# State-space core of a four-layer trunk: output products in 32-column pieces, a new order of products, scans and copies, and two steps of a table computation moved up in the gating layer

## The chip, the cores and the metric

The kernel runs on one core of one Trainium2 chip. The time is that of one execution on the device, in microseconds (us); lower is better. Kernels are compared by the median of several runs on the same chip.

The core's engines work side by side, each on its own queue of instructions in program order: TensorE (PE in the profile, its weight loads PEld), VectorE (DVE), ScalarE (ACT), GpSimd (POOL), and SyncE (SP), which here only issues transfers. An instruction that waits holds up everything behind it on its engine.

## What is computed

The reference is a trunk of four residual layers on 256 tokens of 1024 features in float32. Layer i has a token mixer (attention, spatial gating, state space, attention again) and then a gated MLP with a short convolution. Cut to the two mixers that the change touches:

```python
def chunked_spatial_gating(xn, w_in, v_norm_g, w_s, b_s, w_o):
    u, v = jnp.split(jax.nn.gelu(xn @ w_in), 2, axis=-1)
    v = rmsnorm(v, v_norm_g)              # 128-token chunks, 8 groups
    sv = jnp.einsum('gts,bcsgd->bctgd', jnp.tril(w_s), v) + b_s
    return (u * sv) @ w_o

def s5_layer(xn, w_in, lam_re, lam_im, log_dt, b_re, b_im, c_re, c_im, d_skip, w_glu):
    u = xn @ w_in                         # 64 groups of 16 features, 64 complex states each
    a = exp(dt * (lam_re + 1j * lam_im))  # and bbar from a, lam and b
    x[t] = a * x[t-1] + bbar @ u[t]       # over 256 tokens, by an associative scan
    y = real(c @ x[t]) + d_skip * u[t]
    a, g = jnp.split(gelu(y) @ w_glu, 2, axis=-1)
    return a * sigmoid(g)
```

## The kernel before

Every large product is made of three products of rounded operands (high by high, high by low, low by high): lines 126 to 128 where the weights are loaded into the array and tokens stream, lines 134 to 136 the other way about. A weight chunk of 1 MB comes from memory by an SP transfer (L42) into one of three `raw` buffers; ACT rounds it to the high part (L73, two halves) and DVE subtracts to get the low part (L74, two halves). `prep_to(n)` emits these for all chunks up to n, and `take()` hands out the next chunk. A raw buffer goes to a later chunk once both halves of L74 have read it; the transfer of a chunk is emitted up to two chunks ahead of the one that is being rounded. Chunks marked "tab" are tables of the state-space layer that the kernel has computed itself and stored in memory; they are only transferred (L56).

**The spatial gating layer** (`GMLP`). `body` masks a weight on POOL (L694), makes the last products of v, calls `vnorm` for two halves of the tokens (each has one POOL instruction, L165, for the reciprocal root), and then alternates products (`u`, `sv`, `down`) with `step()`. `step()` rounds weights and takes two steps of a generator, `self.bg`. In this layer that generator is `S5.powers`: powers of the complex decay by repeated squaring, all of it on POOL (L906 to L933), six steps and a closing one. Its scratch tile `powt` lies in the buffer tagged "gb", and that buffer is next given to the norm weights of the following layer (`load_g`, L141). The norm of a layer (`norm`) adds the residual (L192), squares (L153), takes the root on POOL (L165) and scales by these weights (L157); its result is transposed on PE (L181).

**The state-space layer** (`S5`). The 64 groups are 32 pairs. The recurrence is cut into pieces of 4 tokens and 64 chunks. `U` holds the inputs by pair with the 4 tokens side by side (L1240 and L1242 copy it out of the accumulators, 16 copies for each half of the pairs). For four blocks i of eight pairs: `gmm(i)` makes the chunk inputs (L1157), `scan(i)` multiplies by a table of powers, runs two DVE scans (L1175), and multiplies back (L1167 to L1187, some on POOL) to the states x. `kmm(n)` and `kevac(n)` make the short kernel `kk` inside a piece for one half of the pairs (L1196, L1202, and 16 ACT copies at L1206). `ymm(i)` adds three groups of eight products (L1217): `kk` by `U`, and the real and the imaginary states by a table `PP`. Then 16 ACT instructions apply gelu and put the four tokens of a piece into their places (L1224), one copies the high part (L1227), and DVE makes the low part (L1228). `glu(i)` multiplies block i by gate weights into four accumulators; after the fourth, `gate(b)` on ACT and DVE (L1283 to L1285) makes the first half of the output, and four more `glu` make the second.

The tables lie, in the order of their transfers, as bb, p0, gt0, p1, gt1 (`sources`, L752). `gmm` reads gt0 or gt1, `kmm` reads bb and p0 or p1, `ymm` reads p0 or p1. At L1131 `load_t` brings the tables of powers for scans 1 to 3 into the buffers that held the normed input. `mg` (L1107), read by the scans, holds one of the three raw buffers until scan 3 has read it.

The order written out before is: kmm(0); copies of U, the first half on ACT and the second on DVE; gmm(0); scan(0); kevac(0); gmm(1); kmm(1); then for i = 1, 2, 3: scan(i), (kevac(1) after the first), ymm(i-1), gmm(i+1). Gate chunk 0 is rounded ahead of scan(3) (L1250). glu(0), ymm(3), glu(1), glu(2), glu(3) follow, with further chunks rounded by `step()` between them.

Of the kernel before, what the change touches and what calls it, by code (L numbers as in the profile page):

```python
# [8 lines left out]
F32 = mybir.dt.float32  # L9
F32R = mybir.dt.float32r  # L10
BF16 = mybir.dt.bfloat16
AF = mybir.ActivationFunctionType
# [3 lines left out]
D = 1024  # L16
# [600 lines left out]
class GMLP(Phase):  # L617
# [74 lines left out]
    def body(self):  # L692
        k, nc, w = self.k, self.nc, self.k.w
        nc.gpsimd.tensor_tensor(out=self.ws[:, :, :], in0=self.ws[:, :, :],  # L694
                                in1=self.le[:, :].unsqueeze(1).to_broadcast([128, 8, 128]), op=ALU.mult)
        n = w.take()
        for b in range(2):
            k.proj_half(n, 1, b, k.bank(self.vb[b][1]))
        self.v = [self.vnorm(b) for b in range(2)]
        w.step()  # L700

        def step():
            w.step()
            next(self.bg, None)
            next(self.bg, None)

        self.u(0)
        step()
        self.u(1)
        step()  # L710
        self.sv(0)
        self.u(2)
        step()
        self.sv(1)
        self.u(3)
        step()
        self.sv(2)
        k.down(self.gt[0], w.take(), self.acc, (0, 1), True, False)
        step()
        self.sv(3)  # L720
        for _ in self.bg:
            pass
# [11 lines left out]
class S5(Phase):  # L734
# [13 lines left out]
    def sources(self):  # L748
        I = self.k.ins
        o = [(I["ssin"][c], None) for c in range(4)]  # L750
        tab = lambda d, h: lambda: [[d[:, r, h, :]] for r in range(2)]
        t = [lambda: [[self.d_b[:, :]], []], tab(self.d_p, 0), tab(self.d_gt, 0), tab(self.d_p, 1), tab(self.d_gt, 1)]  # L752
        o += [(f, "tab") for f in t]
        return o + [(I["glu"][c], None) for c in range(8)]

# [357 lines left out]
    def body(self):  # L1113
        k, nc, w = self.k, self.nc, self.k.w
        ut = k.pst[:, 4:8, :].rearrange("p b (a t) -> p (b a) t", a=2)
        n = w.take()
# [4 lines left out]
        tabs = [w.take() for _ in range(3)]  # L1121
        TT = []
        for i, tag in enumerate(("xth", "xtl")):
            t = k.big.tile([128, 2048], F32, tag=tag, name=f"T{i}")
# [6 lines left out]
        load_t(slice(0, 512))  # L1131
        tabs += [w.take() for _ in range(2)]
        load_t(slice(512, 1536))
        bb, p0, gt0, p1, gt1 = (w.hl[t] for t in tabs)
        self.kk.append(bb[1][:, :].rearrange("p (a j c) -> p a j c", a=16, j=4))
        nc.gpsimd.memset(bb[1][:, :], 0.0)
        v4 = lambda t: t[:, :].rearrange("p (a c) -> p a c", a=16)
# [1 line left out]
        PP = [[v4(t[r]) for t in (p0, p1)] for r in range(2)]  # L1139
# [1 line left out]
        MG = self.mg[:, :].rearrange("p (a c) -> p a c", a=32)  # L1141
        add, sub, mul = ALU.add, ALU.subtract, ALU.mult
        X, U = {}, []
        gb = lambda i, r: k.bank(((0, 1), (2, 7))[i % 2][r])

# [8 lines left out]
                    o = gb(i, r)[:, 64 * a:64 * a + u.shape[1]]  # L1156
                    nc.tensor.matmul(o, GT[r][pr // 16][:, pr % 16, :], u, start=True, stop=True, skip_group_check=True)  # L1157

        def scan(i):
            ps = slice(8 * i, 8 * i + 8)  # L1160
            b = [gb(i, r).rearrange("p (a c) -> p a c", a=8) for r in range(2)]
            t = [self.tmp.tile([128, 8, 64], F32, tag=f"t{n}", name=f"t{n}") for n in range(4)]
            V, G = nc.vector.tensor_tensor, nc.gpsimd.tensor_tensor
            A = lambda n: t[n][:, :, :]
            T = [self.t0[:, 512 * r:512 * r + 512] if i == 0 else TT[r][:, 512 * (i - 1):512 * i] for r in range(2)]
            T = [v.rearrange("p (a c) -> p a c", a=8) for v in T]
            V(out=A(0), in0=b[0], in1=T[0], op=mul)  # L1167
            V(out=A(1), in0=b[1], in1=T[1], op=mul)
            G(out=A(0), in0=A(0), in1=A(1), op=sub)
            V(out=A(2), in0=b[1], in1=T[0], op=mul)  # L1170
            V(out=A(3), in0=b[0], in1=T[1], op=mul)
            V(out=A(2), in0=A(2), in1=A(3), op=add)
            fl = lambda v: v.rearrange("p a c -> p (a c)")
            for s in (2, 0):
                nc.vector.tensor_tensor_scan(fl(A(s + 1)), fl(MG[:, ps]), fl(A(s)), 0.0, mul, add)  # L1175
            x = X[i] = [self.tmp.tile([128, 8, 64], F32, tag=f"x{r}", bufs=2, name=f"x{r}") for r in range(2)]
            lo, hi = slice(0, 63), slice(1, 64)
            z = [t[1][:, :, lo], t[3][:, :, lo]]
            tr, ti = T[0][:, :, lo], T[1][:, :, lo]
            for r in range(2):  # L1180
                nc.gpsimd.memset(x[r][:, :, 0:1], 0.0)
            V(out=t[0][:, :, lo], in0=z[0], in1=tr, op=mul)
            V(out=t[2][:, :, lo], in0=z[1], in1=ti, op=mul)
            G(out=x[0][:, :, hi], in0=t[0][:, :, lo], in1=t[2][:, :, lo], op=add)
            V(out=x[1][:, :, hi], in0=z[0], in1=ti, op=mul)
            V(out=t[3][:, :, lo], in0=z[1], in1=tr, op=mul)
            G(out=x[1][:, :, hi], in0=t[3][:, :, lo], in1=x[1][:, :, hi], op=sub)  # L1187

        def kmm(n):

            kt = k.bank(3 + n)
            for a in range(4):
                for r in range(2):
                    for q in range(4):
                        pr = 16 * n + 4 * a + q
                        nc.tensor.matmul(kt[32 * q:32 * q + 32, 128 * a:128 * a + 128], BB[r][:, pr, :],  # L1196
                                         PP[r][n][:, pr % 16, :], start=r == 0, stop=r == 1, skip_group_check=True)

        def kevac(n):
            kt = k.bank(3 + n).rearrange("p (a c) -> p a c", a=4)  # L1200
            d = kt[:, :, 0:32]
            nc.vector.tensor_tensor(out=d, in0=d, in1=self.di[:, 4 * n:4 * n + 4], op=add)  # L1202
            kk = self.kk[n][:, :, :, :].rearrange("p (a q) j c -> p q a (j c)", q=4)
            for jp in range(4):
                for q in range(4):
                    nc.scalar.activation(kk[32 * jp:32 * jp + 32, q, :, 32 * jp:128],  # L1206
                                         kt[32 * q:32 * q + 32, :, 0:128 - 32 * jp], AF.Copy)

        def ymm(i):
            p = k.bank(5 + i % 2)  # L1210
            kk, x = self.kk[i // 2], X.pop(i)
            for r in (None, 0, 1):
                for a in range(8):
                    pr = 8 * i + a
                    h, c = pr // 16, pr % 16
                    lhs = kk[:, pr % 16].rearrange("p j c -> p (j c)") if r is None else PP[r][h][:, c, :]
                    nc.tensor.matmul(p[:, 64 * a:64 * a + 64], lhs, U[h][:, c, :] if r is None else x[r][:, a, :],  # L1217
                                     start=a == 0 and r is None, stop=a == 7 and r == 1, skip_group_check=True)
            y = self.tmp.tile([128, 2, 256], F32, tag="y", name="y")
            pv = p.rearrange("p (m r c) -> p m r c", m=2, r=4)  # L1220
            yv = y[:, :, :].rearrange("p m (c j) -> p m c j", j=4)
            for pr in range(4):
                for j in range(4):
                    nc.scalar.activation(yv[32 * pr:32 * pr + 32, :, :, j], pv[32 * j:32 * j + 32, :, pr, :],  # L1224
                                         AF.Gelu_apprx_tanh)
            g = self.gt[i] = k.new_gt()
            nc.scalar.activation(g[0][:, :, :], y[:, :, :], AF.Copy)  # L1227
            nc.vector.tensor_tensor(out=g[1][:, :, :], in0=y[:, :, :], in1=g[0][:, :, :], op=sub)  # L1228

        kmm(0)  # L1230
        for h in range(2):
            u = k.xn_p.tile([128, D], F32, tag="xn", name="U")
            U.append(u[:, :].rearrange("p (a c) -> p a c", a=16))
            d = u[:, :].rearrange("p (m r c) -> p m r c", m=4, r=4)
            for pr in range(4):
                for j in range(4):
                    src = ut[32 * pr:32 * pr + 32, 4 * h:4 * h + 4].rearrange("p m (c j) -> p m c j", j=4)[:, :, :, j]
                    dst = d[32 * j:32 * j + 32, :, pr, :]
                    if h:
                        nc.vector.tensor_copy(dst, src)  # L1240
                    else:
                        nc.scalar.activation(dst, src, AF.Copy)  # L1242
        gmm(0)
        scan(0)
        kevac(0)
        gmm(1)
        kmm(1)
        for i in range(1, 4):
            if i == 3:
                w.prep_to(w.use + 1)  # L1250
            scan(i)
            if i == 1:
                kevac(1)
            ymm(i - 1)
            if i < 3:
                gmm(i + 1)
        acc = [(k.bank(0), k.bank(1)), (k.bank(3), k.bank(4))]
        for i in range(4):
            if i == 1:
                ymm(3)  # L1260
            w.prep_to(w.use + 2)
            self.glu(i, w.take(), acc, (0, 1))
            w.step()
# [111 lines left out]
```

## Time and profile before

| | |
|---|---|
| median of 3 runs | 1237.4 us (1237.31 to 1238.68) |
| the profiled execution | 1238.4 us, its span 1236.6 us |
| DVE, ACT, POOL busy | 892.7 us (72%), 723.1 us (58%), 170.9 us (14%) |
| granted PE clock, mean | 0.981 |
| memory traffic | 239.46 MB, mean 194 GB/s |

Times below are us from the start of the span. "L1157" is line 1157 of the kernel. In a list of instructions a row has the start, the duration, engine, line, operation, operands, and in brackets how long the engine had been idle and what released it. A row of stretches has for each engine the busy time, then the granted clock of PE, the busy share of the transfer engines, and GB/s. A float32 product appears as two records.

### The profile page before, as it was taken

Reading aid. Unit: us, or ns where it says so; the run is one execution under the profiler, and the core shown is the slowest. Engines: PE = TensorE matmul, PEld = TensorE weight load, DVE = VectorE, ACT = ScalarE, POOL = GpSimd, SP = SyncE. Lnnn points to the kernel's source line nnn. Section 1 sums busy time; section 2 is a strip of 40 time slices with the busy share of each in tenths; the row PEclk is TensorE's granted clock in tenths of the full one; section 3 lists DMA queues with packets and bytes.
Section 4 is the critical chain, followed back from the end, with each engine's and each line's share of the span. In section 5 each row is a group of like instructions: output and inputs, shape, how many; then the busy total and the mean of one; then the engine's idle time right before and its main releaser. Section 6 shows DMA issues by size and latency. Waiting matters only on the chain.

```text
span 1236.6 us, 20647 instructions
## 1 busy us (share of the span) xinstructions
PE 1202.4 (97%) x8368; PEld 1106.6 (89%) x8368; DVE 892.7 (72%) x1276; ACT 723.1 (58%) x1120; POOL 170.9 (14%) x314
## 2 busy tenths in 40 slices
PE   8999999999997999999969999999999999999997
PEld 5898999999896999999969789999988988999996
DVE  5665599689855599889485758876766665887673
ACT  5665576467553565576448746655645654665561
POOL 3885000000167000001121000000000000000000
PEclk8999999999999999999978899999999999999999
DMA  8532457877654456668661544655445342465530
GB/s 291 217 108 114 173 198 271 261 250 275 249 195 138 168 219 214 245 253 303 236 256 34 215 180 178 234 201 204 166 158 192 118 151 106 183 232 200 204 121 34
DMA packets 49983, 239.46 MB, mean 194 GB/s; under 512 B 14944, under 2 KB 15840, under 8 KB 24544
## 3 DMA queue, kind: packets, MB, share of 16 engines
q1 hardware_dynamic: 46352, 224.78, 50.0%
q0 software_dynamic: 3392, 13.11, 2.7%
q8 instruction: 65, 1.06, 0.3%
q10 hardware_dynamic: 144, 0.26, 0.1%
q14 instruction: 30, 0.25, 0.1%
HBM read 223.84 MB, written 14.29 MB: 193 GB/s over the span
## 4 chain that ended last, share of the span: by engine, by line
PE 89%; POOL 4%; DVE 3%; issue 1%; DMA 1%; ACT 1%; DVEq 0%; SPq 0%; POOLq 0%; ACTq 0%
PE pst L126 14%; PE pst L128 14%; PE pst L127 14%; PE pst L134 13%; PE pst L135 13%; PE pst L136 13%; PE pst L1217 2%; PE pst L536 1%; PE pst L181 1%; POOL powt L915 1%; DMA gb<-in_g_dram 1%; PE pst L512 1%; PE pst L553 1%; POOL pows L916 1%; DVE wl L70 1%
## 5 line engine op out<-in xcount | busy, mean ns | idle before, releaser
L74 DVE TENSOR_TENSOR wl<-raw,wh 128x1024 fp32r<-128x1024 f32 x344 | 414.1, 1229 | 59.2 <-ACT wh L73 59.1
L126 PE MATMUL pst<-xth,wh 128*128 128x256 f32 x1552 | 441.0, 284 | 0.0
L127 PE MATMUL pst<-xtl,wh 128*128 128x256 f32 x1552 | 439.2, 283 | 0.0
L128 PE MATMUL pst<-xth,wl 128*128 128x256 f32 x1552 | 439.1, 283 | 0.0
L73 ACT ACTIVATE wh<-raw 128x1024 fp32r<-128x1024 f32 x344 | 350.3, 1048 | 13.8 <-DMA raw<-in_glu_dram 6.7
L126 PEld LDWEIGHTS pst<-xth,wh 128*128 128x128 f32 x1552 | 297.7, 192 | 2.3
L127 PEld LDWEIGHTS pst<-xtl,wh 128*128 128x128 f32 x1552 | 297.8, 192 | 1.2
L128 PEld LDWEIGHTS pst<-xth,wl 128*128 128x128 f32 x1552 | 297.7, 192 | 0.0
L410 DVE SCALAR_TENSOR_TENSOR y<-pst,cw,y 128x255 f32<-128x255 f32 x352 | 160.7, 479 | 72.7 <-ACT y L406 66.4
L134 PE MATMUL pst<-wh,gh 128*128 128x512 f32 x512 | 202.9, 396 | 0.0
L135 PE MATMUL pst<-wl,gh 128*128 128x512 f32 x512 | 201.0, 393 | 0.0
L136 PE MATMUL pst<-wh,gl 128*128 128x512 f32 x512 | 200.7, 392 | 0.0
L406 ACT ACTIVATE y<-pst,cw 128x256 f32<-128x256 f32 x176 | 88.0, 556 | 69.3 <-PE pst L128 64.7
L136 PEld LDWEIGHTS pst<-wh,gl 128*128 128x128 f32 x512 | 96.8, 189 | 21.2 <-DVE gl L1228 0.4
L134 PEld LDWEIGHTS pst<-wh,gh 128*128 128x128 f32 x512 | 97.3, 190 | 19.8 <-issue 0.3
L135 PEld LDWEIGHTS pst<-wl,gh 128*128 128x128 f32 x512 | 97.2, 190 | 18.4
L134 PE MATMUL pst<-wh,xth 128*128 128x256 f32 (+1 forms) x336 | 105.9, 315 | 0.0
L136 PE MATMUL pst<-wh,xtl 128*128 128x256 f32 (+1 forms) x336 | 105.3, 313 | 0.0
L135 PE MATMUL pst<-wl,xth 128*128 128x256 f32 (+1 forms) x336 | 105.3, 313 | 0.0
L165 POOL TENSOR_TENSOR r<-m,mhalf 128x1 f32<-128x1 f32 x20 | 11.1, 554 | 681.3 <-DVE m L163 681.2
L416 ACT ACTIVATE y<-y 128x256 f32<-128x256 f32 x88 | 36.4, 419 | 78.3 <-DVE y L410 78.3
L200 ACT ACTIVATE gh<-y 128x256 fp32r<-128x256 f32 x88 | 36.1, 418 | 75.4 <-DVE y L417 75.4
(180 smaller groups left out, 1282.8 us busy)
## 6 DMA issues: line engine op xcount, KB each, us to landing
raw<-in_up_dram SPq DMA_DIRECT2D x88, 1024.0 KB, 5.0
raw<-in_down_dram SPq DMA_DIRECT2D x44, 1024.0 KB, 4.8
raw<-in_wqk_dram SPq DMA_DIRECT2D x16, 1024.0 KB, 4.9
raw<-in_wo_dram SPq DMA_DIRECT2D x8, 1024.0 KB, 4.8
raw<-in_glu_dram SPq DMA_DIRECT2D x8, 1024.0 KB, 6.3
raw<-in_wv_dram SPq DMA_DIRECT2D x7, 1024.0 KB, 4.9
gb<-in_g_dram SPq DMA_DIRECT2D x9, 512.0 KB, 5.8
d_gt<-gf POOLq DMA_DIRECT2D x4, 1024.0 KB, 7.5
```

What stands on the lines that cost most here:

```text
L73: nc.scalar.activation(h[:, s], r[:, s], AF.Copy)
L74: nc.vector.tensor_tensor(out=l[:, s], in0=r[:, s], in1=h[:, s], op=ALU.subtract)
L126: nc.tensor.matmul(out, h[:, cols], xh, start=first, stop=False, skip_group_check=True)
L127: nc.tensor.matmul(out, h[:, cols], xl, start=False, stop=False, skip_group_check=True)
L128: nc.tensor.matmul(out, l[:, cols], xh, start=False, stop=last, skip_group_check=True)
L134: nc.tensor.matmul(out, ah, h[:, cols], start=first, stop=False, skip_group_check=True)
L135: nc.tensor.matmul(out, ah, l[:, cols], start=False, stop=False, skip_group_check=True)
L136: nc.tensor.matmul(out, al, h[:, cols], start=False, stop=last, skip_group_check=True)
L200: self.nc.scalar.activation(g[0][:, j], src, AF.Copy)
L406: nc.scalar.activation(y[:, cs], p[:, cs], AF.Identity, scale=cw[:, s, m, 2:3], bias=cw[:, s, m, 3:4])
L410: nc.vector.scalar_tensor_tensor(y[:, o + tap:o + 256], p[:, o:o + 256 - tap], cw[:, s, m, 2 - tap:3 - tap], y[:, o + tap:o + 256], ALU.mu ...
L416: nc.scalar.activation(y[:, 256:512], y[:, 256:512], AF.Silu)
```

## The change

Five edits. In `GMLP.body`, two steps of the generator are taken right after the mask, ahead of `vnorm`. In `S5.sources`, the tables come as gt0, p0, bb, gt1, p1. `gmm(1)` writes banks 2 and 5 instead of 2 and 7. `ymm` is split into products and evacuation: each product with 128 columns of weights becomes four with 32, placed so that the four tokens of a piece lie along the free axis and the features along the partitions; `yevac` then needs one gelu instead of 16. The 16 copies of U are a function, `ucopy(h, halves)`: with `halves` those of odd pr go to DVE, without it all go to ACT. And the order of everything in `S5.body` after the tables is written anew.

```diff
 GMLP.body
         nc.gpsimd.tensor_tensor(out=self.ws[:, :, :], ...)
+        for _ in range(2):
+            next(self.bg, None)
         n = w.take()
 S5.sources
-        t = [lambda: [[self.d_b[:, :]], []], tab(self.d_p, 0), tab(self.d_gt, 0), tab(self.d_p, 1), tab(self.d_gt, 1)]
+        t = [tab(self.d_gt, 0), tab(self.d_p, 0), lambda: [[self.d_b[:, :]], []], tab(self.d_gt, 1), tab(self.d_p, 1)]
 S5.body
-        gb = lambda i, r: k.bank(((0, 1), (2, 7))[i % 2][r])
+        gb = lambda i, r: k.bank(((0, 1), (2, 5), (0, 1), (2, 7))[i][r])
...
-        def scan(i):
+        def scan(i, mid=lambda: None):
...
             V(out=A(3), in0=b[0], in1=T[1], op=mul)
+            mid()
             V(out=A(2), in0=A(2), in1=A(3), op=add)
...
+        def kd(n):
+            d = k.bank(3 + n).rearrange("p (a c) -> p a c", a=4)[:, :, 0:32]
+            nc.vector.tensor_tensor(out=d, in0=d, in1=self.di[:, 4 * n:4 * n + 4], op=add)
...
-        def ymm(i):
-            p = k.bank(5 + i % 2)
-            kk, x = self.kk[i // 2], X.pop(i)
-            for r in (None, 0, 1):
-                for a in range(8):
...
-                    nc.tensor.matmul(p[:, 64 * a:64 * a + 64], lhs, U[h][:, c, :] if r is None else x[r][:, a, :],
-                                     start=a == 0 and r is None, stop=a == 7 and r == 1, skip_group_check=True)
+        def ymm(i, parts):
+            p, h = k.bank(6 - i % 2), i // 2
+            for r in parts:
+                for m in range(2):
+                    for j in range(4):
+                        for q in range(4):
+                            a = 4 * m + q
+                            c = 8 * (i % 2) + a
+                            lhs = self.kk[h][:, c, j, :] if r is None else PP[r][h][:, c, 32 * j:32 * j + 32]
+                            nc.tensor.matmul(p[32 * q:32 * q + 32, 256 * m + 64 * j:256 * m + 64 * j + 64], lhs,
+                                             U[h][:, c, :] if r is None else X[i][r][:, a, :],
+                                             start=r is None and m == 0 and j == 0, stop=r == 1,
+                                             skip_group_check=True)
+
+        def yevac(i):
+            p = k.bank(6 - i % 2)
             y = self.tmp.tile([128, 2, 256], F32, tag="y", name="y")
-            for pr in range(4):
-                for j in range(4):
-                    nc.scalar.activation(yv[32 * pr:32 * pr + 32, :, :, j], pv[32 * j:32 * j + 32, :, pr, :],
-                                         AF.Gelu_apprx_tanh)
+            nc.scalar.activation(y[:, :, :].rearrange("p m (c j) -> p m j c", j=4),
+                                 p.rearrange("p (m j c) -> p m j c", m=2, j=4), AF.Gelu_apprx_tanh)
...
+        def ucopy(h, halves):
...
                     dst = d[32 * j:32 * j + 32, :, pr, :]
+                    if halves and pr % 2:
                         nc.vector.tensor_copy(dst, src)
                     else:
                         nc.scalar.activation(dst, src, AF.Copy)
...
+        K_, X_ = (None,), (0, 1)
+        ucopy(0, True)
         gmm(0)
+        w.prep_to(w.use + 1)
+        ucopy(1, False)
+        kmm(0)
+        kmm(1)
         gmm(1)
+        def lags():
+            for n in range(2):
+                kd(n)
+                kevac(n)
+        scan(0, lags)
+        gmm(2)
+        ymm(0, K_)
+        scan(1)
+        ymm(0, X_)
+        yevac(0)
+        gmm(3)
+        ymm(1, K_ + X_)
+        scan(2)
+        yevac(1)
+        ymm(2, K_)
+        w.prep_to(w.use + 2)
+        scan(3)
         acc = [(k.bank(0), k.bank(1)), (k.bank(3), k.bank(4))]
+        self.glu(0, w.take(), acc, (0, 1))
+        ymm(2, X_)
+        yevac(2)
+        w.prep_to(w.use + 2)
+        ymm(3, K_)
+        self.glu(1, w.take(), acc, (0, 1))
+        ymm(3, X_)
+        yevac(3)
+        for i in (2, 3):
             w.prep_to(w.use + 2)
             self.glu(i, w.take(), acc, (0, 1))
             w.step()
```

More of the change, by code (lines that the diff above doesn't have):

```diff
@@ L1133, in body @@
         load_t(slice(512, 1536))
-        bb, p0, gt0, p1, gt1 = (w.hl[t] for t in tabs)
+        gt0, p0, bb, gt1, p1 = (w.hl[t] for t in tabs)
         self.kk.append(bb[1][:, :].rearrange("p (a j c) -> p a j c", a=16, j=4))
@@ L1197, in kmm @@
                                          PP[r][n][:, pr % 16, :], start=r == 0, stop=r == 1, skip_group_check=True)
+        def kd(n):
+            d = k.bank(3 + n).rearrange("p (a c) -> p a c", a=4)[:, :, 0:32]
+            nc.vector.tensor_tensor(out=d, in0=d, in1=self.di[:, 4 * n:4 * n + 4], op=add)
         def kevac(n):
             kt = k.bank(3 + n).rearrange("p (a c) -> p a c", a=4)
-            d = kt[:, :, 0:32]
-            nc.vector.tensor_tensor(out=d, in0=d, in1=self.di[:, 4 * n:4 * n + 4], op=add)
             kk = self.kk[n][:, :, :, :].rearrange("p (a q) j c -> p q a (j c)", q=4)
@@ L1207, in kevac @@
                                          kt[32 * q:32 * q + 32, :, 0:128 - 32 * jp], AF.Copy)
-        def ymm(i):
-            p = k.bank(5 + i % 2)
-            kk, x = self.kk[i // 2], X.pop(i)
-            for r in (None, 0, 1):
-                for a in range(8):
[L1214 to L1217, printed above, removed]
-                                     start=a == 0 and r is None, stop=a == 7 and r == 1, skip_group_check=True)
-            y = self.tmp.tile([128, 2, 256], F32, tag="y", name="y")
-            pv = p.rearrange("p (m r c) -> p m r c", m=2, r=4)
-            yv = y[:, :, :].rearrange("p m (c j) -> p m c j", j=4)
-            for pr in range(4):
-                for j in range(4):
-                    nc.scalar.activation(yv[32 * pr:32 * pr + 32, :, :, j], pv[32 * j:32 * j + 32, :, pr, :],
-                                         AF.Gelu_apprx_tanh)
+        def ymm(i, parts):
[13 more added lines that the diff above has]
+            p = k.bank(6 - i % 2)
+            y = self.tmp.tile([128, 2, 256], F32, tag="y", name="y")
+            nc.scalar.activation(y[:, :, :].rearrange("p m (c j) -> p m j c", j=4),
+                                 p.rearrange("p (m j c) -> p m j c", m=2, j=4), AF.Gelu_apprx_tanh)
             g = self.gt[i] = k.new_gt()
@@ L1228, in ymm @@
             nc.vector.tensor_tensor(out=g[1][:, :, :], in0=y[:, :, :], in1=g[0][:, :, :], op=sub)
[L1230 to L1234, printed above, removed]
+        def ucopy(h, halves):
+            d = U[h].rearrange("p (m r) c -> p m r c", m=4)
             for pr in range(4):
@@ L1238, in body @@
                     dst = d[32 * j:32 * j + 32, :, pr, :]
-                    if h:
+                    if halves and pr % 2:
                         nc.vector.tensor_copy(dst, src)
@@ L1242, in body @@
                         nc.scalar.activation(dst, src, AF.Copy)
+        for h in range(2):
+            U.append(k.xn_p.tile([128, D], F32, tag="xn", name="U")[:, :].rearrange("p (a c) -> p a c", a=16))
+        K_, X_ = (None,), (0, 1)
+        ucopy(0, True)
         gmm(0)
-        scan(0)
-        kevac(0)
+        w.prep_to(w.use + 1)
+        ucopy(1, False)
+        kmm(0)
+        kmm(1)
         gmm(1)
[L1247 to L1256, printed above, removed]
-        acc = [(k.bank(0), k.bank(1)), (k.bank(3), k.bank(4))]
-        for i in range(4):
-            if i == 1:
-                ymm(3)
+        def lags():
[15 more added lines that the diff above has]
+        scan(3)
+        acc = [(k.bank(0), k.bank(1)), (k.bank(3), k.bank(4))]
+        self.glu(0, w.take(), acc, (0, 1))
[7 more added lines that the diff above has]
+        for i in (2, 3):
             w.prep_to(w.use + 2)
```

## The prediction

> **What bounds the kernel now.** The page's first section says that PE is busy for nearly the whole span, so I looked for the places where it is not: the row of slices, then stretches around the two dips, then the waits and the lists by engine there.
>
> ```profile
> PE 1202.4 (97%) x8368; PEld 1106.6 (89%) x8368; DVE 892.7 (72%) x1276; ACT 723.1 (58%) x1120; POOL 170.9 (14%) x314
> ```
>
> The first dip is at the end of the gating layer. PE stands still for 6.65 us and then runs at half clock:
>
> ```profile
> 392.80:399.50 6.70, 0.07 (x1) 0.00 (x0) 0.80 (x2) 0.00 (x0) 2.00 (x3) 0.83 0.71 187
> 399.50:403.90 4.40, 4.39 (x15) 3.81 (x16) 4.09 (x5) 1.19 (x2) 0.00 (x0) 0.50 1.00 415
> ...
> 399.51 1.97 PE L181 MATMUL pst<-ident,xn 128*128 128x128 f32 x8 [6.65 <-DVE xn L157]
> ...
> DVE xn L157 <- DMA gb<-in_g_dram: 8.5, 1, 8.5
> ...
> SPq L141 <- POOL pows L933: 17.1, 1, 17.1
> ```
>
> PE waits for the scaled input (L157), that for the norm weights (gb), and their transfer for POOL to finish the powers whose scratch holds the buffer. POOL's list shows how long that takes, and that it was free for 17.33 us before:
>
> ```profile
> 346.25 0.55 POOL L165 TENSOR_TENSOR r<-m,mhalf 128x1 f32<-128x1 f32 x1 [17.33 <-DVE m L163]
> ...
> 349.77 2.43 POOL L915 TENSOR_TENSOR powt<-pows,spar 128x32 f32<-128x32 f32 x2
> ...
> 353.52 0.50 POOL L915 TENSOR_TENSOR powt<-pows,spar 128x32 f32<-128x32 f32 x2
> ...
> 357.72 0.57 POOL L915 TENSOR_TENSOR powt<-pows 128x64 f32<-128x64 f32 x2
> ...
> 391.05 2.52 POOL L933 TENSOR_TENSOR pows<-pows,powt 128x512 f32<-128x512 f32 x2
> ...
> 390.00 0.21 DVE L163 TENSOR_SCALAR m<-ss 128x1 f32<-128x1 f32 x1 [0.81 <-ACT xn L153]
> ```
>
> Steps one and two of the generator run from 349.77 to 357.72, with two memsets ahead of them; the whole ends at 393.57, 3.6 us after DVE had the norm's sum ready (390.0).
>
> The second dip is the core of the state-space layer, 616 to 694:
>
> ```profile
> 616.10:643.30 27.20, 15.93 (x230) 14.93 (x229) 22.30 (x37) 12.09 (x30) 5.36 (x8) 0.87 0.73 289
> 643.30:653.50 10.20, 10.19 (x48) 10.20 (x49) 2.86 (x4) 7.58 (x19) 2.65 (x2) 0.50 0.01 3
> 658.60:664.00 5.40, 5.40 (x51) 5.40 (x51) 3.06 (x5) 2.23 (x6) 1.03 (x1) 1.00 0.00 0
> 664.00:667.50 3.50, 3.50 (x33) 3.50 (x33) 3.40 (x5) 3.26 (x9) 0.34 (x3) 1.00 0.02 5
> 683.30:693.90 10.60, 10.55 (x42) 9.68 (x43) 8.84 (x8) 3.92 (x5) 1.47 (x1) 0.53 0.59 233
> 693.90:708.40 14.50, 14.50 (x63) 11.45 (x62) 7.74 (x8) 14.27 (x25) 0.00 (x0) 0.99 0.48 173
> ...
> 708.41 0.39 PE L136 MATMUL pst<-wh,gl 128*128 128x512 f32 x1
> ```
>
> PE idles for 11 of the 27 us before 643.3 and does all of ymm(0) at half clock (0.50 to 653.5); ymm(1), from 658.6, and gmm(3), from 664, are at full clock, and after 683 the clock is halved again. Both delays are chains on ACT and DVE:
>
> ```profile
> 617.47 6.19 ACT L1242 ACTIVATE U<-pst 32x256 f32<-32x256 f32 x16 [3.65 <-PE pst L368]
> 637.03 7.06 ACT L1206 ACTIVATE kk<-pst 32x512 f32<-32x512 f32 x16 [13.37 <-POOL x L1184]
> 653.82 6.42 ACT L1224 ACTIVATE y<-pst 32x128 f32<-32x128 f32 x16 [0.55 <-PE pst L1217]
> 660.27 0.63 ACT L1227 ACTIVATE gh<-y 128x512 fp32r<-128x512 f32 x1
> ...
> 627.52 0.69 DVE L1167 TENSOR_TENSOR t<-pst,t 128x512 f32<-128x512 f32 x1
> 636.59 0.29 DVE L1202 TENSOR_TENSOR pst<-pst,di 128x128 f32<-128x128 f32 x1
> 660.94 0.69 DVE L1228 TENSOR_TENSOR gl<-y,gh 128x512 fp32r<-128x512 f32 x1 [14.78 <-ACT gh L1227]
> ```
>
> A scan is 9.07 us of DVE (627.52 to 636.59). DVE then lies idle for 14.78 us behind ACT's copies and 16 gelus. From 683 on PE has almost no gap; the last product of glu(3) starts at 708.41, so that the next glu begins at 708.6.
>
> **The change part by part.** *Powers.* The two steps, 357.72 - 349.77 = 8 us, move into POOL's idle 17.33 us. The last one then ends near 393.6 - 8 = 385.6, and the weights (5.01 us by the chain of waits below) land at 390.6. Next late is the root on POOL at 390.8 and L157 at 390.9; its halves are done by 391.6 and 392.3, just when PE arrives at 392.87 (399.51 - 6.65). So the whole hole goes: 6.65 us idle, and half of the 4.4 us at clock 0.50, 2.2. **Gain 8.8 us**, between 0 and 8.8. It stays whole if the powers end before about 387.
>
> ```profile
> 393.60 5.01 DMA gb<-in_g_dram
> ```
>
> *Pieces.* `kmm` has the only products with 32 columns now: 64 records from 620.40 to 622.28, 0.0294 us each. Today's `ymm` has 16 records in 1.79 us (the next 16 start at 660.37), 0.112 each. One `ymm` goes from 48 x 0.112 = 5.4 us to 192 x 0.0294 = 5.64 us at full clock: four cost 1.1 us more. Bounds: 0.028 (a quarter) and 0.112 (no overlap of the four column strips); I take `kmm`'s row, the same form.
>
> ```profile
> 620.40 0.43 PE L1196 MATMUL pst<-wh,wh 128*32 128x128 f32 x8
> 622.28 0.47 PE L1157 MATMUL pst<-U,wh 128*128 128x112 f32 x2
> ...
> 658.58 1.95 PE L1217 MATMUL pst<-U,kk 128*128 128x64 f32 x16
> 660.37 1.95 PE L1217 MATMUL pst<-x,wh 128*128 128x64 f32 x16
> ```
>
> The evacuation falls from 6.42 to one gelu of 128x512. L1227's 0.63 is the nearest row, four times L1224's 0.40 the upper bound; I take 0.65. That is 5.8 us of ACT saved per block.
>
> *The early rounding of gate chunk 0.* On ACT it now stands ahead of the second half's U copies, on DVE ahead of scan(0). Both wait for its transfer:
>
> ```profile
> 624.79 0.93 SPq L42 DMA_DIRECT2D raw<-in_glu_dram  x2
> ...
> raw<-in_glu_dram SPq DMA_DIRECT2D x1, 1024.0 KB, 17.0
> ...
> raw<-in_glu_dram SPq DMA_DIRECT2D x1, 1024.0 KB, 4.8
> ...
> 671.22 1.99 ACT L73 ACTIVATE wh<-raw 128x1024 fp32r<-128x1024 f32 x2
> ...
> 672.37 2.35 DVE L74 TENSOR_TENSOR wl<-raw,wh 128x1024 fp32r<-128x1024 f32 x2
> ```
>
> The 17.0 are its time to landing (the 4.8 that of a chunk issued alone, at 697). SP issues it behind `load_t` and both late tables, 5.5 MB that cannot start before the input products end at 620.4, where `kmm` starts. The change moves none of that, so the chunk lands again at 624.79 + 17.0 = 641.8 (I keep the old time axis in this stage). ACT: rounding to 643.8, second U copies (6.19) to 650.0, kevac(0) (7.06) to 657.0, kevac(1) to 664.1. DVE: low part from 642.9 to 645.3, scan(0) with two `kd` of 0.29 to 654.9, scan(1) to 664.0. Scan(0) thus starts 17.8 us later than today. PE waits for kk at 657.0.
>
> From there PE is the late one. DVE goes on behind the first gelu (ymm(0) done at 665.6, low part by 667.6): scan(2) to 676.7, low part 1 and chunk 1 to 681.1, scan(3) to 690.2; POOL ends a block's states some 1.2 to 1.6 us later, so 665, 678 and 692 for blocks 1 to 3. ymm(1), the state parts of ymm(2) and those of ymm(3) come on PE at 670, 683 and 695. PE has 4 x 5.64 (ymm) + 3.6 (gmm(3): 33 records in 3.50 us from 664.0, with one or so of its neighbours) + 4 x 5.5 (glu: 24 products at 14.50 / 63 = 0.23) = 48.2 us of work, of which I put 0.8 us of first pieces before 657.0. At full clock glu(3) would end at 704.4; today it is 708.6. The clock takes that back. Before 657 PE has been idle for most of 12 us, and today's row shows ymm(0) at half clock for all its 10.2 us; it was released only in the wider gmm(2). The pieces stream the same 64 columns, so I take the same: half clock from 658 through the rest of ymm(0) into gmm(3), to about 668.5, 10.4 us at half speed = 5.2 us. **glu(3) ends at 709.6**, 1.0 later than today.
>
> *The end of the stage.* Today chunks 1 to 4 are rounded before `yevac(3)`. Now chunks 3 to 7 all stand between it and `gate`. Let T be the end of ymm(3). ACT has gelu and copy to T+1.3, chunk 3 to T+3.3 (DVE done T+4.8), chunks 4 and 5 to T+7.3. Chunk 6 needs the raw buffer of chunk 3: issued at T+4.8, landed 4.8 later, rounded by T+11.6; chunk 7, issued at T+7.2, by T+14.0. Then the sigmoid's table, the sigmoid and a multiply, 2.8 us today (708.44 to 711.21): banks 0 and 1 are free at T+16.8.
>
> ```profile
> 708.44 1.28 ACT L1283 ACT_TABLE_LOAD   x1
> ...
> 710.53 0.68 DVE L1284 TENSOR_TENSOR gate<-pst,gate 128x512 f32<-128x512 f32 x1
> ...
> 711.36 0.41 PE L134 MATMUL pst<-wh,gh 128*128 128x512 f32 x1
> ```
>
> PE needs these banks after two and a half glu's, T+13.6; today it went on at 711.36, without a wait. **Loss 3.2 us**, between 0 (if chunks land at once) and 5 (if the clock drops in the gap).
>
> The new order of tables and bank 5 cost nothing: gt0 arrives before it is needed, kmm(1) and gmm(1) wait for p1 in PE's idle time, at most until 641.8, when chunk 0 behind it has landed, and scan(1) wants gmm(1) at 654.9. If scan(0) did not wait for chunk 0 that cover would be gone, and p1 would be late instead by up to some 6 us.
>
> **Sum:** -8.8 + 1.0 + 3.2 = -4.6 us, made against the profiled execution (1238.4; span 1236.6, 1.8 around it). From the median, 1237.4, it is **1232.8 us**.
>
> **Rivals.** *The pieces wake the clock.* Four strips keep some product streaming nearly all the time; what the gate counts, no row here shows. Restarted by wide products at 399.5 it was released after 4.4 us. If ymm(0) does the same, the cold time is some 3.5 us, costing 1.8 instead of 5.2: -8.0, **1229.4**. Against it speaks the long half clock from 643.3 to 653.5. The Trainium skill, "TensorE: Matmul & The Clock Gate", Part 1, says that a window of about 3.4 us of sustained activity gives full clock; by that rule this rival would be the outcome, while the 10.2 us here show that not every busy PE counts.
>
> *The powers gain nothing* (the slower side). The moved steps meet six L74 in a row:
>
> ```profile
> 332.45 6.90 DVE L74 TENSOR_TENSOR wl<-raw,wh 128x1024 fp32r<-128x1024 f32 x6 [0.26 <-ACT wh L73]
> ```
>
> Two POOL instructions took 2.43 us beside DVE's work at 349.77 that took 0.50 at 353.52. If the 22 moved instructions take twice their 8 us, they pass 346.25 and hold up the v norm. Once the powers end past 387, each us costs one, and past 391.6 the kernel is slower. With all gone: +4.2, **1241.6**. The Trainium skill, "SBUF — State Buffer", Who interferes with whom, has a lock that blocks POOL for the whole of a DVE instruction with two SBUF inputs; L74 (6.90 / 6 = 1.2 us) is one, so 22 waits of that length are an estimate of 26 us at worst.
>
> *The pieces put the clock down* in the later blocks, too. Today's ymm at full clock kept it (658.6 to 664). If four narrow strips count for less, ymm(1) to ymm(3) (16.9 us) run partly at half speed, 6 (a third of it) to 17 us (all) more, say 10: **1242.8**.
>
> *Chunk 0 is no wait* (the order or the transfer is not what I read): scan(0) starts 17.8 us earlier and all behind it, 1232.8 - 17.8 = **1215**.
>
> **How the numbers follow.** Forecast 0.47, clock woken 0.25, powers without gain 0.10, clock put down 0.13, no wait 0.05. The range leaves out the last, and the far half of the clock put down: 1227 to 1242. Faster by over 0.2% (2.5 us, what a measurement of this kernel can tell from none): 0.38 of the forecast, all of the first and the last, 0.68. Within: 0.09 + 0.07 of the two slow cases, 0.16. Slower: 0.16.
>
> **What would show it.** Powers end near 385 and PE has no hole before L181. ACT idles before its first L73 of chunk 0 for some 20 us until about 633 on the new axis (8.8 earlier), scan(0) begins near 636.5, PE restarts near 648 at half clock. One gelu per block, 0.65. PE waits some 3 us inside the first glu after `gate`. If scan(0) starts near 617, or ymm costs far from 5.64, the sum is wrong.

## The result, and the profile after

The changed kernel takes **1230.88 us** (median of 4 runs, 1229.20 to 1231.62), the kernel before, run beside it, 1237.95 (4 runs). The ratio is 0.9941, its 95% interval 0.9924 to 0.9958: 7.1 us less, 0.6%. The forecast was 1232.8, its range 1227 to 1242. The profiled execution took 1229.2 us (span 1227.4); it is the shortest of the four. Already at 325 us, where nothing is changed yet, it is 1.0 us ahead of the old one, so a difference of 1 us between two traces says nothing.

The page's busy times of the changed kernel, and the two stretches in which PE stood still and then ran at half clock before:

```profile
PE 1191.1 (97%) x8944; PEld 1092.2 (89%) x8944; DVE 893.1 (73%) x1268; ACT 706.4 (58%) x1068; POOL 173.2 (14%) x314
```

```profile
392.80:399.50 6.70, 6.70 (x43) 5.97 (x42) 5.14 (x8) 2.88 (x7) 0.04 (x1) 1.00 0.50 172
399.50:403.90 4.40, 4.40 (x40) 4.40 (x39) 1.41 (x2) 0.96 (x2) 0.52 (x1) 1.00 0.00 0
```

The hole is gone, and so is the half clock behind it. PE's busy total fell by 11.3 us (1202.4 before). The lists by engine in the gating layer of the changed kernel:

```profile
327.84 0.21 POOL L908 MEMSET pows<- 128x64 f32 x1
...
342.80 0.30 POOL L926 TENSOR_TENSOR pows<-powt 128x32 f32<-128x32 f32 x1
345.16 0.55 POOL L165 TENSOR_TENSOR r<-m,mhalf 128x1 f32<-128x1 f32 x1 [2.07 <-DVE m L163]
...
378.06 3.00 POOL L935 TENSOR_TENSOR pows<-pows,powt 128x512 f32<-128x512 f32 x2
```

```profile
378.19 1.72 DVE L690 TENSOR_TENSOR gl<-t,gh 128x512 fp32r<-128x512 f32 x1 [0.69 <-ACT gh L689]
379.83 3.45 DVE L74 TENSOR_TENSOR wl<-raw,wh 128x1024 fp32r<-128x1024 f32 x2
...
390.62 0.21 DVE L163 TENSOR_SCALAR m<-ss 128x1 f32<-128x1 f32 x1 [0.81 <-ACT xn L153]
391.52 1.42 DVE L157 SCALAR_TENSOR_TENSOR xn<-x,r,gb 128x512 f32<-128x512 f32 x2 [0.69 <-POOL r L165]
```

```profile
385.32 0.50 PE L134 MATMUL pst<-wh,gh 128*128 128x512 f32 x1 [1.64 <-ACT gh L689]
```

The two moved steps take 15.3 us in their new place (327.84 to 343.1; 8 before), but POOL is free again before the v norm asks for it, at 345.16. The powers end at 381.06, 12.5 earlier than before (1.0 of it is the lead that the trace has already at 325 us). Now POOL's last, widest instructions lie beside the DVE work that prepares the last products of the layer. The same two rows of the kernel before:

```profile
378.25 0.69 DVE L690 TENSOR_TENSOR gl<-t,gh 128x512 fp32r<-128x512 f32 x1 [0.70 <-ACT gh L689]
379.19 2.58 DVE L74 TENSOR_TENSOR wl<-raw,wh 128x1024 fp32r<-128x1024 f32 x2 [0.26 <-ACT wh L73]
```

L690 has gone from 0.69 to 1.72 us, the pair of L74 from 2.58 to 3.45, and PE has a new gap of 1.64 us, at 385.32. In the kernel before, PE was busy all through that stretch:

```profile
384.00:392.80 8.80, 8.80 (x40) 7.00 (x38) 5.15 (x6) 4.94 (x8) 8.46 (x7) 1.00 0.00 0
```

The core of the state-space layer, ACT and DVE of the changed kernel:

```profile
633.16 2.00 ACT L73 ACTIVATE wh<-raw 128x1024 fp32r<-128x1024 f32 x2 [18.69 <-DMA raw<-in_glu_dram]
635.19 6.20 ACT L1247 ACTIVATE U<-pst 32x256 f32<-32x256 f32 x16
641.41 7.22 ACT L1211 ACTIVATE kk<-pst 32x512 f32<-32x512 f32 x16
...
655.72 1.19 ACT L1232 ACTIVATE y<-pst 128x512 f32<-128x512 f32 x1
```

```profile
634.25 2.36 DVE L74 TENSOR_TENSOR wl<-raw,wh 128x1024 fp32r<-128x1024 f32 x2 [17.99 <-ACT wh L73]
636.64 0.69 DVE L1169 TENSOR_TENSOR t<-pst,t 128x512 f32<-128x512 f32 x1
...
658.21 0.68 DVE L1169 TENSOR_TENSOR t<-pst,T 128x512 f32<-128x512 f32 x1
...
671.10 0.68 DVE L1169 TENSOR_TENSOR t<-pst,T 128x512 f32<-128x512 f32 x1
```

Both engines wait some 18 us for gate chunk 0, and scan(0) begins at 636.64, scan(2) at 658.21, scan(3) at 671.10. Late in the stage DVE is busy for 27.32 of the 29.40 us from 657.6 to 687.0, PE only for 22.36. The stretches ahead of it show where PE was cold, in gmm(2) until 646.7, and that ymm(0), which follows, was not:

```profile
639.20:646.70 7.50, 7.28 (x32) 6.97 (x32) 7.43 (x11) 7.16 (x17) 2.30 (x5) 0.50 0.22 90
646.70:649.20 2.50, 2.40 (x67) 1.56 (x70) 2.46 (x4) 2.35 (x7) 1.88 (x4) 0.98 0.01 3
657.60:687.00 29.40, 22.36 (x465) 18.23 (x466) 27.32 (x31) 10.43 (x12) 8.84 (x10) 0.90 0.27 94
```

On PE, the pieces of ymm(1), then the waits late in the stage:

```profile
654.86 1.10 PE L1224 MATMUL pst<-U,kk 128*32 128x64 f32 x64
655.78 1.08 PE L1224 MATMUL pst<-x,wh 128*32 128x64 f32 x64
...
679.81 1.10 PE L1224 MATMUL pst<-x,wh 128*32 128x64 f32 x64 [2.91 <-POOL x L1187]
...
702.05 0.50 PE L134 MATMUL pst<-wh,gh 128*128 128x512 f32 x1 [2.52 <-DVE gate L1311]
```

64 records in 0.92 us are 0.0144 us each, half of `kmm`'s 0.0294. PE waits for the states that the scans make (2.91 us at 679.81) and at the end for `gate` (2.52 us).

### The profile page after: what moved, and what is told of

The parts are those of the page before. It is cut to its first block, busy times and chain, and to the rows that moved or that the text cites. A ratio compares the mean times of both kernels' runs of the same rounds, so it can differ in the third digit from the quotient of the medians.

```text
span 1227.4 us, 21740 instructions
## 1 busy us (share of the span) xinstructions
PE 1191.1 (97%) x8944; PEld 1092.2 (89%) x8944; DVE 893.1 (73%) x1268; ACT 706.4 (58%) x1068; POOL 173.2 (14%) x314
## 4 chain that ended last, share of the span: by engine, by line
PE 89%; DVE 5%; DMA 2%; ACT 2%; issue 1%; SPq 0%; POOL 0%; DVEq 0%; POOLq 0%; ACTq 0%
PE pst L126 15%; PE pst L128 15%; PE pst L127 15%; PE pst L134 13%; PE pst L136 13%; PE pst L135 13%; DMA raw<-in_glu_dram 2%; PE pst L536 1%; DVE wl L74 1%; PE pst L181 1%; PE pst L512 1%; PE pst L553 1%; DVE wl L70 1%; DVE t L1178 1%; DMA x<-in_x_dram 1%
## 5 line engine op out<-in xcount | busy, mean ns | idle before, releaser
L74 DVE TENSOR_TENSOR wl<-raw,wh 128x1024 fp32r<-128x1024 f32 x344 | 417.4, 1238 | 75.8 <-ACT wh L73 75.8
```

What stands on the lines that cost most here:

```text
L74: nc.vector.tensor_tensor(out=l[:, s], in0=r[:, s], in1=h[:, s], op=ALU.subtract)
```

## The experiments

Medians; the kernel before ran beside each group of runs and took between 1236.9 and 1238.0 us, so medians of two groups compare to about 1 us. "After" is the changed kernel, 1230.9.

**Taking the change apart.** `powers_only` is the kernel before with one edit, and `core_only` is the changed kernel without it:

```diff
 GMLP.body
+        for _ in range(2):
+            next(self.bg, None)
```

> The kernel before, with nothing of the change but the two steps of the powers moved up in the gate. Forecast on record: 8.8 us less than before. Theory from the trace of after (POOL's last 128x512 instructions of the powers now run beside VectorE's chain at the start of the layer, and that chain begins 1.6 us later than it could): 6.3 to 7.3 us less. Rival (the steps gain nothing on their own): within 1 us of before.

Measured: 1231.07 against 1237.84, ratio 0.9944 (0.9932 to 0.9957): 6.8 us less.

> The changed kernel without the two moved steps: the powers end as late as before. Theory from the trace of after (the 64-column pieces cost 0.0141 us, so the new stage is a little shorter than the old one): 0.5 to 2.5 us less than before. Forecast on record for this part: 4.2 us more than before (1.0 in the stage, 3.2 at the gate that ends it).

Measured: 1238.91 (11 runs) against 1237.84, ratio 1.0006 (0.9997 to 1.0015). PE's hole is where it was:

```profile
399.13 1.12 PE L181 MATMUL pst<-ident,xn 128*128 128x128 f32 x4 [6.63 <-DVE xn L157]
```

So the gain is that of the powers. The rest of the change, all of its rewriting of the core, is worth nothing that can be measured (0.4 less to 1.9 more); my reading of a gain from one trace missed as the forecast's 4.2 us loss did. What remained was to find why so large a rewrite does nothing.

**How the powers gain.** `one_step` takes one step of the generator ahead, not two.

> The kernel before with one step of the powers moved up instead of two. Theory that the gain is only that POOL's queue is free when the layer's first reciprocal root comes (390.9 us in after, POOL done at 381.4): one step of some 5 to 6 us is about enough, 5.0 to 6.5 us less than before (6.8 with two steps). Rival that the gain goes with the work moved: about 3.4 us less. Second rival, that POOL's last 128x512 instructions beside VectorE's chain cost what they overlap (now more of it): 2 to 4 us less, with VectorE's norm work at 380 to 390 us longer than in after.

Measured: 1231.78 against 1237.33, 0.9952 (0.9939 to 0.9964): 5.6 us less with half the work moved. Its POOL and DVE rows:

```profile
384.66 2.97 POOL L935 TENSOR_TENSOR pows<-pows,powt 128x512 f32<-128x512 f32 x2
...
384.80 1.69 DVE L690 TENSOR_TENSOR gl<-t,gh 128x512 fp32r<-128x512 f32 x1 [0.69 <-ACT gh L689]
386.41 3.44 DVE L74 TENSOR_TENSOR wl<-raw,wh 128x1024 fp32r<-128x1024 f32 x2
...
391.86 0.21 DVE L163 TENSOR_SCALAR m<-ss 128x1 f32<-128x1 f32 x1 [0.81 <-ACT xn L153]
```

POOL ends 6.6 us later than in after, and the long DVE instructions moved with it: in after the L690 of 378 us took 1.72, here the next one, of 384.80, takes 1.69. That ties them to POOL's wide instructions. The gain hangs on POOL being done when the layer's norm needs it, not on the amount moved.

**The wait for the transfer.** `late_round` moves the rounding of gate chunk 0 from ahead of scan(0) to behind scan(1):

```diff
         gmm(0)
-        w.prep_to(w.use + 1)
         ucopy(1, False)
...
         scan(1)
+        w.prep_to(w.use + 1)
         ymm(0, X_)
```

> The changed kernel with the rounding of gate chunk 0 moved from behind the first 112-column products to behind scan(1), so that neither ScalarE nor VectorE stands before scan(0) waiting for the transfer. Theory that the scans on VectorE and POOL set the end and the transfer holds scan(0): the time falls by 5 to 10 us below the changed kernel's. Rival that TensorE sets the end (the price of the pieces and the half clock): within 2 us of the changed kernel. Second rival, that something else that ScalarE and VectorE wait for (kmm(1), which has the second powers table only at 627 to 630 us) takes the place of the wait: 2 to 5 us less.

Measured: 1223.61, 0.9886 (0.9872 to 0.9899): 7.3 us less than after. `early_dma` leaves the rounding where it is and issues the chunk's transfer sooner (`dma_to` gets an argument that lets it pass the tables):

```diff
+        w.dma_to(w.use + 3, True)
         load_t(slice(0, 512))
```

> The changed kernel with the transfer of gate chunk 0 issued ahead of the first pair of the table transfers (T) instead of behind them. In the trace of after the wait for this chunk is 18.7 us on ScalarE and 18.0 us on VectorE. Theory that the scans are the chain that sets the end: scan(0) starts 8 to 17 us sooner and the time falls by 6 to 12 us below the changed kernel's. Rival that TensorE sets the end: within 2 us. Rival that the T transfers, now later, hold scan(1) instead: 0 to 3 us less.

Measured: 1221.27, 0.9866 (0.9853 to 0.9880): 9.6 us less than after. Two edits that have only the 18 us wait in common each gain as the scan theory said; PE is busy for 1190 to 1191 us in all three. Both edits free ACT as well as DVE, so they don't tell which of the two waits counted. Neither gets all 18, and both stop at the same place, the second `kd`, which waits for kmm(1) and so for table p1 (first row `late_round`, second `early_dma`):

```profile
631.21 0.30 DVE L1204 TENSOR_TENSOR pst<-pst,di 128x128 f32<-128x128 f32 x1 [7.52 <-PE pst L1199]
```

```profile
634.46 0.30 DVE L1205 TENSOR_TENSOR pst<-pst,di 128x128 f32<-128x128 f32 x1 [7.40 <-PE pst L1200]
```

`split_lags` is `late_round` with that wait taken out of scan(0). It makes two moves at once, which were not taken apart: `kd(1)` with its copies goes into scan(1), and gmm(1) ahead of kmm(1):

```diff
         kmm(0)
-        kmm(1)
         gmm(1)
+        kmm(1)
...
-        def lags():
-            for n in range(2):
-                kd(n)
-                kevac(n)
+        def lags(n):
+            kd(n)
+            kevac(n)
-        scan(0, lags)
+        scan(0, lambda: lags(0))
...
-        scan(1)
+        scan(1, lambda: lags(1))
```

> The kernel with the late rounding, and two moves more: the second half of the evacuation (kd(1), kevac(1)) goes from scan(0) into scan(1), and gmm(1) goes ahead of kmm(1). In the trace of late_round VectorE waits 7.5 us in kd(1) for kmm(1), whose table lands at about 630 us, and is then busy without a gap until 678 us. Theory that VectorE's chain sets the end: 4 to 8 us less than late_round (1223.6), so 1215.5 to 1219.5. Rival that TensorE has become the bound once the wait for the transfer is gone: within 1.5 us of late_round.

Measured: 1218.01, 0.9845 (0.9832 to 0.9858), 5.6 us less than `late_round`. The wait in `kd(1)` is down to 0.79 us:

```profile
633.25 0.30 DVE L1204 TENSOR_TENSOR pst<-pst,di 128x128 f32<-128x128 f32 x1 [0.79 <-PE pst L1199]
```

**The price of a piece.** `strips` exchanges two loops, so that four products in a row go to one group of 32 partitions instead of to four:

```diff
-                    for j in range(4):
-                        for q in range(4):
+                    for q in range(4):
+                        for j in range(4):
```

> The changed kernel with the two inner loops of the pieces exchanged, so that four products in a row write the same 32 partitions instead of four different groups of 32. Nothing else differs. Theory that products to four different groups overlap, and that this makes a record cost 0.0141 us: 64 records take about 3.6 us instead of 0.9, the stage's TensorE work grows by some 30 us, and the kernel becomes 10 to 30 us slower than the changed one. Rival that 0.0141 us is what 64 columns cost in any order: 64 records still take 0.9 us and the time stays within 2 us.

> The kernel strips again, timed: its records cost 0.030 us instead of 0.0141, which is the price (0.0294) that the forecast took for the pieces. Theory that this price was the forecast's error in the stage: with it the kernel takes 4 to 7 us more than the changed one, 1235 to 1238, and its stage is about as far above the stage of before as the forecast's 4.2 us. Rival that the single time of strips (1236.3) was a scatter: 1230 to 1233.

Measured: 1236.26 in the one run, then 1237.18 (10 runs) against 1237.50, ratio 0.9998 (0.9989 to 1.0007): 6.3 us slower than after. The pieces of its ymm(1) on PE, in the timed run:

```profile
661.17 2.05 PE L1224 MATMUL pst<-x,wh 128*32 128x64 f32 x58
663.01 0.24 PE L1224 MATMUL pst<-x,wl 128*32 128x64 f32 x1
```

From 661.17 to 663.01 there are 58 records, 0.032 us each, 2.2 times the 0.0144 of after. So the order matters, but by a factor of 2.2 and not the 4 that I expected, and the loss is smaller than the 10 us that I gave as the least. The Trainium skill, "TensorEngine Tiling (Array Packing)", Key Properties, says that the four tiles of 128x32 operate independently; taken alone that would make the rotating order four times as fast, and the runs show 2.2.

**The half clock.** `warm` does gmm(1) a second time where PE idles for 5.4 us ahead of gmm(2):

```diff
         scan(0, lags)
+        gmm(1)
         gmm(2)
```

> The changed kernel with gmm(1) done twice, the second time in front of gmm(2), where TensorE idles 5.4 us and then runs at half clock; the result is the same, the work is 4.5 us more. Theory that TensorE's half clock in gmm(2) and the first pieces is off the path, since VectorE's scans set the end: within 1.5 us of the changed kernel, with or without a full clock in gmm(2). Rival that the half clock costs time: 2 to 4 us less if the repeated products bring the full clock ahead of gmm(2), or 2 to 5 us more if they do not.

Measured: 1230.58, 0.9943 (0.9929 to 0.9957): the same as after. The half clock only moved, to some 643 to 650 us:

```profile
646.00:649.40 3.40, 3.40 (x18) 3.38 (x16) 3.40 (x5) 3.25 (x7) 2.09 (x2) 0.50 0.01 2
```

So 3.6 us more of PE's work (the second gmm(1) runs at full clock from 636.66 on, and is shorter than the 4.5 that I gave) cost nothing. PE is not what that part of the stage waits for.

**The end of the stage.** `gate_first` is `split_lags` with the last rounding of the loop behind the gates, and `gate_only` makes the same edit in the changed kernel:

```diff
-        for i in (2, 3):
-            w.prep_to(w.use + 2)
-            self.glu(i, w.take(), acc, (0, 1))
-            w.step()
+        w.prep_to(w.use + 2)
+        self.glu(2, w.take(), acc, (0, 1))
+        w.step()
+        n = w.take()
+        self.glu(3, n, acc, (0, 1))
         for b in range(2):
             self.gate(b, acc[b], k.x[:, b, 0:512])
+        w.step()
```

> split_lags with one more move: the rounding that the last step of the stage's loop issues (in split_lags ScalarE at 684.6 us, behind a wait of 1.8 us for its transfer) goes behind the two gates. In split_lags TensorE then waits 4.7 us for the gates. Theory that this rounding stands ahead of the table load and the sigmoid and so makes that wait: the wait shrinks to 1 to 2 us and the kernel takes 2.5 to 4 us less, 1214 to 1215.5. Rival that the rounded chunk is late next, or that the sigmoids wait for their products anyway: within 1 us of split_lags (1218.0).

Measured: 1211.57, 0.9795 (0.9782 to 0.9808), 6.4 us less than `split_lags`; I expected up to 4. PE's wait for the gates in `split_lags` and in `gate_first`, and then the stretches around it in `split_lags`:

```profile
689.28 0.79 PE L134 MATMUL pst<-wh,gh 128*128 128x512 f32 x1 [4.67 <-DVE gate L1310]
```

```profile
684.39 0.50 PE L134 MATMUL pst<-wh,gh 128*128 128x512 f32 x1 [0.80 <-DVE gate L1312]
```

```profile
684.00:687.40 3.40, 0.62 (x3) 0.19 (x1) 1.94 (x3) 2.79 (x3) 0.00 (x0) 1.00 0.98 378
687.40:690.80 3.40, 1.52 (x4) 1.23 (x5) 2.84 (x5) 3.39 (x6) 0.00 (x0) 0.54 0.73 251
690.80:694.20 3.40, 3.40 (x10) 2.63 (x9) 3.40 (x4) 2.58 (x5) 0.00 (x0) 0.50 0.79 328
```

The wait is 3.9 us shorter. Behind the long wait the clock was halved, too: 4.9 us of PE's time (1.52 + 3.40) ran at half speed, 2.5 us lost. Together 6.4. In `gate_first` the clock stays full behind the short wait:

```profile
686.00:690.00 4.00, 4.00 (x19) 3.28 (x18) 4.00 (x5) 3.16 (x4) 0.00 (x0) 1.00 0.40 152
```

> The changed kernel with one edit: the rounding that the last step of the stage's loop issues goes behind the two gates. In the trace of after TensorE waits 2.52 us for the gates and keeps its full clock. Theory that this rounding makes the wait, and that the 6.4 us of gate_first were 4.7 us of wait plus a half clock that followed it there: here 1.5 to 2.8 us less than the changed kernel (1230.9). Rival that the edit brings some 6 us wherever it is made: 5 us less or more. Rival that the wait has another cause: within 1 us.

Measured: 1225.98, 0.9908 (0.9892 to 0.9925), 4.9 us less than after: more than I gave, and so near the rival's 5 that it is not excluded, since two groups compare to about 1 us. PE's wait of 2.52 us for the gates is gone. The two traced executions, 1229.2 and 1225.9 us, are only 3.3 apart; what else differs between them shows most in one stretch ahead of the gates, first after, then `gate_only`:

```profile
672.00:690.00 18.00, 14.10 (x169) 11.35 (x168) 16.03 (x17) 7.97 (x10) 4.42 (x5) 0.81 0.50 177
```

```profile
672.00:690.00 18.00, 14.16 (x174) 11.51 (x173) 16.02 (x18) 7.97 (x10) 4.43 (x5) 0.91 0.49 176
```

The program is the same in that stretch, and the clock was granted differently: about 3.6 us less at half speed, some 1.8 us of work. This is not the scatter of one execution: the mean granted clock is 0.988 to 0.989 in all four of `gate_only` and 0.986 to 0.987 in all four of after. Why the clock differs ahead of the edit stays open, and so does how much of the 4.9 us is due to the shorter wait alone.

**One more that does nothing.** `p1_first` is `gate_first` with p1 fetched ahead of gt1.

> gate_first with the second powers table (p1) fetched ahead of the second gain table (gt1). In split_lags kmm(1) waits 2.8 us for p1 and VectorE and ScalarE are 0.8 to 2.8 us late behind it. Theory that VectorE's chain still sets the end: 1 to 2.5 us less than gate_first. Rival that gmm(2), which needs gt1, takes the wait over, or that TensorE's own work is now the bound: within 0.7 us, or up to 2 us more.

Measured: 1211.38, 0.9797 (0.9783 to 0.9810): no difference; the 1 to 2.5 us of my theory did not come. What holds `gate_first` now was not looked for. `gate_first`, the simpler of the two, beats both kernels of this case: 2.05% below the kernel before and 19.3 us below the changed one.

## Why the prediction was nearly right, point by point

The time was inside the range and on the forecast side, but two terms were wrong, in opposite directions: the powers gained 2.0 us less than forecast, and the core lost 3.5 us less. That these largely cancel is luck.

- **Powers, -8.8: the mechanism was right, the size was -6.8.** The hole went as described. The forecast left out what POOL's last instructions would then meet: 1.64 us of PE's time. 8.8 - 1.64 = 7.2, inside the interval of `powers_only`. The premise of the second rival came true (15.3 us for the moved steps, about twice 8, and well under the 26 given as the worst), but POOL's idle time was long enough for it. The prediction could have seen that: twice 8 is 16, and POOL was idle for 17.33 us ahead of 346.25.
- **Chunk 0: right.** ACT idle for 18.69 us until 633.16, scan(0) at 636.64; the forecast said some 20, about 633, and 636.5. The rival without a wait is out. The runs show what that wait was worth: 7 to 10 us, not the 17.8 that the rival's sum gave it, because p1 is next, the "some 6 us" that the forecast named (7.5 measured).
- **The step that failed: "From there PE is the late one".** It rested on a piece at `kmm`'s 0.0294 us, so 5.64 us for one `ymm`. Measured are 0.0144, so 192 x 0.0144 = 2.8; four `ymm` are 11.5 us shorter than I had them at full clock, and 10.5 shorter than before (4 x 5.4). In `core_only`, where the powers are as before, PE's busy total is 1194.2 us, 8.2 less than before. `kmm`'s products stream 128 columns and the pieces 64, and I took the row for its form and passed over the width. My lower bound of 0.028 was wrong for another reason: the old `ymm` streams 64 columns as well, but the records of `gmm`, which stream 112, take about as long as its 0.112 (33 in the 3.50 us from 664.0 that the prediction shows, 0.106). So that price does not go with the streamed columns, and a quarter of it is no bound for pieces whose price does. With a price near mine, in `strips`, the kernel is 6.3 us slower than after and its core 6.5 us worse than the old one (-0.3 without the powers' -6.8), against the 4.2 of the forecast. There PE waits for none of the states, while in after it waits 5.3 us for them: in after, DVE's chain of scans is late instead. Of the 6.3 us, 2.2 are a longer wait for the gates (4.7 us in `strips`). My times for it held: scan(2) starts at 658.21 and scan(3) at 671.10, where 667.6 and 681.1 less 8.8 were forecast.
- **The clock: wrong place.** I had ymm(0) at half clock; gmm(2) was cold instead, and ymm(0) ran at full clock from 646.7. `warm` shows that it did not matter, because of the point before. Another half clock comes late, behind the 2.91 us wait; since PE waits 2.52 us for the gates after it all the same, what it costs in after is not shown.
- **The gate, +3.2: there, measured 2.52.** One gelu is 1.19 us in the row above, not 0.65, still far below the 16 that took 6.42.
- **The core's sum, +4.2: measured 0.7 more (0.4 less to 1.9 more).** `late_round` and `gate_only` show that it is a balance: the new order could gain, but the wait for chunk 0 holds it back by some 7 us and the gates by 2.5 to 5. Of what gains in it, `strips` shows the price of the pieces alone; the single gelu, the order of the tables and the bank were not taken apart.

## What to carry to other kernels

A rewrite that only breaks even may be paying for its gain with a wait that it set itself: here two moves of a rounding step, one to behind the scans and one to behind the gates, and a split of the copies turned 0.6% into 2%. Before an instruction that waits for a transfer is put ahead of a chain, look up when the transfer can land and what is queued behind it on that engine. When a duration is borrowed from another line, compare the streamed width and the order of the products too, and write down what will be late if the price turns out half as large.

## What the runs showed of the hardware

The granted clock changes at regular points. In the trace of after, cut into stretches of 3.41 us from 616.02 on, it changes only at their borders:

```profile
626.26:629.67 3.41, 2.54 (x48) 2.36 (x52) 0.00 (x0) 0.00 (x0) 0.00 (x0) 0.51 1.03 412
629.67:633.09 3.42, 3.42 (x43) 3.21 (x34) 0.00 (x0) 0.00 (x0) 0.00 (x0) 0.99 1.01 423
...
639.91:643.32 3.41, 3.21 (x16) 2.94 (x15) 3.34 (x5) 3.28 (x8) 0.00 (x0) 0.50 0.23 99
643.32:646.74 3.42, 3.42 (x17) 3.32 (x16) 3.42 (x5) 3.25 (x8) 2.17 (x2) 0.50 0.03 7
...
677.45:680.87 3.42, 1.06 (x64) 0.94 (x64) 3.42 (x6) 0.00 (x0) 2.05 (x2) 1.00 0.83 304
680.87:684.28 3.41, 2.42 (x69) 2.20 (x66) 3.19 (x3) 0.37 (x1) 0.98 (x1) 0.51 0.03 7
684.28:687.69 3.41, 3.41 (x9) 2.65 (x8) 1.75 (x2) 3.38 (x5) 0.00 (x0) 0.50 0.73 262
687.69:691.11 3.42, 3.42 (x16) 2.76 (x15) 3.42 (x4) 3.42 (x4) 0.00 (x0) 0.99 0.41 103
...
697.93:701.35 3.42, 1.60 (x8) 0.98 (x6) 2.41 (x3) 3.39 (x5) 0.00 (x0) 1.00 0.93 338
701.35:704.76 3.41, 2.71 (x12) 2.26 (x13) 3.34 (x5) 2.78 (x4) 0.00 (x0) 1.00 0.92 322
```

The stretch in which PE was busy for 1.06 us is followed by two at half clock, the one with 1.60 us by full clock. So the wait of 2.91 us, most of it inside one stretch, cost two stretches at half speed, and the 2.52 us of the gates, partly in one stretch and partly in the next, cost only themselves. What brings the clock back is not settled by these rows: it came back behind a half-clock stretch with 2.54 us of PE, and not behind one with 3.21. The Trainium skill, "TensorE: Matmul & The Clock Gate", Part 1, describes a free-running window of 3413 ns, which agrees.

Where the borders lie differs between the kernels: in `gate_only` the changes of this stage come 1.2 us later than in after, while the two traces of `strips` agree to 0.2 us. Executions of one kernel can differ, too: the mean granted clock of `split_lags` was 0.990 in two of them (1218.9 and 1220.1 us) and 0.993 in the other three (1217.9 to 1218.0 us).
